# Six of eight units of a gate pair by seven products, a token sum in x's place, and a new order of the accumulating loads

## The chip, the cores and the metric

The kernel runs on one core of a Trainium2 chip. The time is device microseconds of one execution. A core has TensorE (PE, matmul; PEld is its weight load), VectorE (DVE), ScalarE (ACT), GpSimd (POOL) and SyncE (SP), each with its own instruction queue that runs in order. DMAs are issued here from SP's, ScalarE's and POOL's queues.

## What is computed

One layer of a decoder trunk on 256 tokens and 2048 features, in float32: a combined projection of the normed x, a short convolution branch and a gated recurrence branch, and then two sigmoid gates that merge the branches:

```python
h = rmsnorm(x, norm_mix_g[i])
u = h @ w_in[i]
...
m = jax.nn.sigmoid(ga) * (ya @ w_a_out[i]) + jax.nn.sigmoid(gb) * (yb @ w_b_out[i])
x = x + m @ w_o[i]
gate = jax.nn.sigmoid(rmsnorm(x, ple_norm_g[i]) @ w_ple_gate[i])
x = x + gate * (p[i] @ w_ple_proj[i])
```

ga and gb are two column ranges of u, 2048 columns each. The change is in how `h @ w_in` is computed for them.

## The kernel before

**Split operands.** A float32 product is made of three matmuls in the float32r format: each operand is cut in a high part (ScalarE copies it, rounded) and a low part (VectorE subtracts), and `triple` runs high x high, high x low and low x high. `cut` (L163 to L166) does this for a weight tile of 128 x 1024: `whi` by ScalarE, `wlo` by VectorE. x is cut once, into the two tiles of `state["hT"]` (16 slices of 128 features, 256 tokens each), which stay.

**Steps.** The projections run as a list of steps (`items`). A plain step takes one chunk of 256 features by 512 columns: 2 feature slices x 2 token halves x 3 = 12 matmuls. At step n the loop splits the weights of step n + 3 (`LEAD`), issues the matmuls of step n, issues loads up to step n + 7, and lets every open epilogue (a generator) go one step on. Weights come in tiles `raw` from SP's queue; the split pairs `whi`, `wlo` turn in four buffers.

**Pairs of gates.** The columns of ga and gb are done in four groups j of 512. After both gates of a j come the groups A and B (four plain steps each), whose results are multiplied in by `ep_a` and `ep_bb` and added into m. For j = 0 both gates are plain groups of eight steps. For the three later j the two gates are computed as a pair: a unit is one chunk of 256 features for both gates, so a product of a 2 x 2 block matrix (token halves by feature slices) with another (feature slices by gates). A unit with eight products is two steps of kind C, 12 matmuls each. A unit in `SEVEN` is one step of kind S that needs only seven products, 21 matmuls, by the scheme of Strassen and Winograd, but has sums of weights and of tokens as operands.

- Weights, `combine_weights` (L180): tile `sA` holds the unit's weights for ga, `sB` the second half of those for gb, both loaded from SP's queue (two buffers each). Tile `sT` holds the gb weights plus another block, and this sum is made by POOL's queue: a plain DMA, then an accumulating one (`add_by_dma`, three buffers). VectorE makes two sums in place in `sA` (L696), and three cuts follow: `thi`, `tlo` of sT (operands t1, t3), `bhi`, `blo` of sB (operand b22), `thi`, `tlo` of sA (t2, t4). The pairs `thi`, `tlo` turn in three buffers and `bhi`, `blo` has one. The plain split of sA into `whi`, `wlo` comes ahead of the sums. `combine_weights` for step n + 2 is issued at step n, ahead of the split of step n + 3.
- Tokens, `token_sums` (L730): for each unit in SEVEN, four sums s1 to s4 of the blocks of x are made and cut once, after group ga of j = 0, in groups of one or two units (`TOGETHER`), in a few steps of gb, A and B of j = 0; all three pairs use them.
- Products, `unit_products`: the seven go to the banks of `names_of`, in that order; `ep_products` and `ep_gates` put the banks together behind the last unit.

**Order.** From the end of ga of j = 0 until the end of the last B, `pinned` holds the instructions of ScalarE and of VectorE to the order in which the code issues them. In that order, at the last step of a group B, stand: the combination for step n + 2, the split of step n + 3, and then the four instructions of `ep_bb`, which wait for that step's matmuls. The end of a pair's last unit is followed directly by group A.

The other place that the change touches is `third_part`, in the third last step of the first group of W_o: it opens the tile for the sum x + m W_o, and `residual(0)` loads the first 512 columns of x into it from SP's queue.

Of the kernel before, what the change touches and what calls it, by code (L numbers as in the profile page):

```python
# [9 lines left out]
F32 = mybir.dt.float32  # L10
F32R = mybir.dt.float32r
AF = mybir.ActivationFunctionType
ALU = mybir.AluOpType
PSUM = bass.MemoryType.PSUM

P = 128
# [7 lines left out]
CW = 512  # L24
# [4 lines left out]
LB_MAX = 1.0 - 1e-6  # L29
SCAN = 64  # L30
LEVELS = [32, 16, 8, 4]
SEVEN = [()] + 3 * [(0, 2, 3, 5, 6)]
TOGETHER = [(0, 1), (1, 2), (3, 2)]
NARROW, Q = len(LEVELS), 32


# [11 lines left out]
def hybrid_kernel(ctx, tc, xT, x, pT, prm, gfin, masks, w_in, w_a, w_b, w_o, w_pg, w_pp, out):  # L48
    nc = tc.nc
# [9 lines left out]
    pools, closers = {}, {}  # L59

    def open_pool(name, side):
        closers[name] = ExitStack()
        pools[name] = closers[name].enter_context(
            tc.tile_pool(name=name, bufs=1, side=side, reuse_waits="tile")
        )

    def close_pool(name):
        closers.pop(name).close()
        del pools[name]
# [3 lines left out]
    state = {"tmp": "tmp1"}  # L73
# [3 lines left out]
    def nm(s):  # L77
        uid[0] += 1
        return f"{s}_{uid[0]}"
# [8 lines left out]
    def sc(n, tag="sc", bufs=12):  # L88
        return small.tile([P, n], F32, tag=tag, bufs=bufs, name=nm(tag))
# [6 lines left out]
    pair_sums = {}  # L96
# [9 lines left out]
    items = []  # L106
    for gi, (kind, j, w, g, op) in enumerate(groups):
        if kind == "gb" and SEVEN[j]:
            continue
        for c in range(w.shape[2]):  # L110
            it = {"gi": gi, "kind": kind, "j": j, "c": c, "last": c == w.shape[2] - 1}
            if kind != "ga" or not SEVEN[j]:
                key = ("PP", j // 2) if kind == "PP" else (gi, c // 2)
                items.append(dict(it, w=(w, g, c), raw=key, slot=(j if kind == "PP" else c) % 2))
            elif c in SEVEN[j]:
                items.append(dict(it, kind="S", w=(w, g, c), raw=(gi, c)))
# [6 lines left out]
    def raw_of(pos):  # L123
        it = items[pos]
        if it["raw"] not in loaded:
            if it["kind"] == "S":
                t = tuple(
                    pools["st"].tile([P, n, CW], F32, tag=tag, bufs=2, name=nm(tag)) for tag, n in (("sA", 2), ("sB", 1))
                )
            else:  # L130
                t = wp.tile([P, 2, 2 * CW], F32, tag="raw", bufs=3, name=nm("raw"))
            loaded[it["raw"]] = t
        return loaded[it["raw"]]
# [15 lines left out]
            else:  # L149
                nc.sync.dma_start(out=raw, in_=w[g, :, c : c + 2, :])  # L150

    def add_by_dma():
        pos = next((n for n, it in enumerate(items) if it["kind"] == "S" and n not in pair_sums), None)
        if pos is not None:
            w, g, c = items[pos]["w"]
            X = pair_sums[pos] = pools["st"].tile([P, 2, CW], F32, tag="sT", bufs=3, name=nm("sT"))
            nc.gpsimd.dma_start(out=X.rearrange("p n x -> p (n x)"), in_=w[g + 1, :, c, :])
            nc.gpsimd.dma_start(out=X, in_=w[g : g + 2, :, c, :CW].rearrange("n p x -> p n x"), accum_op=ALU.add)

    def pair_of(pool, n, tags=("whi", "wlo"), width=2 * CW):  # L160
        return tuple(pool.tile([P, width], F32R, tag=tag, bufs=n, name=nm(tag)) for tag in tags)
# [18 lines left out]
    def combine_weights(pos):  # L180
        st = pools["st"]
        (A, B), X = raw_of(pos), pair_sums[pos]
        add(A[:, 0], X[:, 0], B[:, 0])
        add(A[:, 1], A[:, 0], A[:, 1])
        ts = []
        for n, src in enumerate((X, B, A)):
            hi, lo = pair_of(st, 1, ("bhi", "blo"), CW) if n == 1 else pair_of(st, 3, ("thi", "tlo"))
# [9 lines left out]
    begun = next(n for n, it in enumerate(items) if it["kind"] == "ga" and it["last"])  # L197
# [7 lines left out]
    prm_t = const.tile([P, PRM_N], F32, name="prm_t")  # L205
    praw = pools["tmp1"].tile([P, 1024], F32, tag="X", bufs=4, name="praw")[:, : 2 * T]
    pop = pools["tmp1"].tile([P, 1024], F32R, tag="X", bufs=4, name="pop")
# [487 lines left out]
    def add(out, a, b):  # L695
        nc.vector.tensor_tensor(out=out, in0=a, in1=b, op=ALU.add)  # L696
# [32 lines left out]

    def token_sums():  # L730
        nu = len(SEVEN[1])
        state["S"] = pair_of(pools["st"], 1, ("shi", "slo"), nu * 4 * P)
        state["S"] = tuple(v.rearrange("p (u s t) -> p u s t", u=nu, s=4) for v in state["S"])
        for first, n in TOGETHER:
            for _ in range(3):
                yield
            F, S = (
                pools["st"].tile([P, 2 * CW], F32R, tag=tag, bufs=3, name=nm(tag))[:, : n * 4 * P].bitcast(F32)
                for tag in ("thi", "tlo")
            )  # L740
            c = SEVEN[1][first]
            hi, lo = (v[:, 2 * c : 2 * (c + n), :] for v in state["hT"])
            Fv = F.rearrange("p (k t) -> p k t", t=T)
            nc.vector.tensor_tensor(out=Fv, in0=hi.bitcast(F32), in1=lo.bitcast(F32), op=ALU.add)
            yield
            Fv = F.rearrange("p (u r b t) -> p u r b t", u=n, r=2, b=2)
            Sv = S.rearrange("p (u s t) -> p u s t", u=n, s=4)
            a11, a12, a21, a22 = Fv[:, :, 0, 0], Fv[:, :, 1, 0], Fv[:, :, 0, 1], Fv[:, :, 1, 1]
            s1, s2, s3, s4 = (Sv[:, :, i] for i in range(4))
            for out, u, v, op in (  # L750
                (s1, a21, a22, ALU.subtract), (s2, s1, a11, ALU.subtract),
                (s3, a11, a21, ALU.subtract), (s4, a12, s2, ALU.add),
            ):
                nc.vector.tensor_tensor(out=out, in0=u, in1=v, op=op)
            hi, lo = (v[:, first : first + n] for v in state["S"])
            nc.scalar.activation(out=hi, in_=Sv, func=AF.Copy)
            nc.vector.tensor_tensor(out=lo, in0=Sv, in1=hi.bitcast(F32), op=ALU.subtract)
            yield

    def ep_a(j, psum):  # L760
# [219 lines left out]
        open_pool("tmp2", "right")  # L980
        state["tmp"] = "tmp2"

    def residual(j):

        for t in range(NT):
            s = slice(j * CW, (j + 1) * CW)
            nc.sync.dma_start(out=state["x"][:, t, s], in_=x[:, t, s])

    def load_gfin():
        g = state["gfin"] = pools["tmp3"].tile([P, D], F32, name="gfin_t")  # L990
# [5 lines left out]
    def third_part():  # L996

        close_pool("tmp2")
        close_pool("branch")
        open_pool("tmp3", "right")  # L1000
        state["tmp"] = "tmp3"
        xs = pools["tmp3"].tile([P, NT, D], F32, name="xs")
        state["x"] = xs
        residual(0)
        state["ss2"] = sc(8, "ss2", 1)
        state["ss3"] = sc(12, "ss3", 1)
        nc.gpsimd.memset(state["ss3"].rearrange("p (t j) -> p t j", t=NT)[:, :, 5:6], EPS)
# [14 lines left out]
    def finish():  # L1022
        while active:
            advance()
# [24 lines left out]
    def names_of(it):  # L1049
        if it["kind"] == "C":  # L1050
            return [("c", it["n"], t) for i in range(2) for t in range(NT)]
        return ["P1", ("c", 0, 0), ("c", 1, 0), "P5", "P7", "P6", ("c", 0, 1)]

    def into(name, op, part):
        left[name] -= 1
# [3 lines left out]
    def unit_products(pos):  # L1059
        it = items[pos]  # L1060
        c, h = it["c"], state["hT"]

        def x_of(r, t):
            return tuple(v[:, 2 * c + r, t * P : (t + 1) * P] for v in h)

        hi, lo = parts.pop(pos)
        halves = [(hi[:, i * CW : (i + 1) * CW], lo[:, i * CW : (i + 1) * CW]) for i in range(2)]
        names = names_of(it)
        if it["kind"] == "C":
            for n, name in enumerate(names):  # L1070
                into(name, x_of(n // 2, n % 2), halves[n // 2])
            return
        b22, t1, t3, t2, t4_ = sums.pop(pos)
        s1, s2, s3, s4 = (tuple(v[:, SEVEN[1].index(c), i] for v in state["S"]) for i in range(4))
        for name, op, part in zip(names, (x_of(0, 0), x_of(1, 0), s4, s1, s3, s2, x_of(1, 1)),
                                  (halves[0], halves[1], b22, t1, t3, t2, t4_)):
            into(name, op, part)

    def pinned(start):
# [16 lines left out]
    for pos, it in enumerate(items[:last_group]):  # L1096
        mark = len(nc.cur_bb.bb.instructions)
        kind, j, c, last = (it[n] for n in ("kind", "j", "c", "last"))
        _, _, w, g, opname = groups[it["gi"]]
# [60 lines left out]
        else:  # L1160
            if c == 0:
                psum = [bank("s" if kind == "PP" and j >= 2 else "g") for _ in range(NT)]
            hi, lo = parts.pop(pos)
            for i in range(2):
                k = 2 * c + i
                s = slice(i * CW, (i + 1) * CW)
# [10 lines left out]
        if pos == begun:  # L1177
            finish()
            second_part()
            active.append(token_sums())  # L1180
            for _ in range(3):
                add_by_dma()
        if kind == "O" and j == 0 and c == nch - 3:
            finish()
            third_part()
# [22 lines left out]
    for t, halves in ((0, (0, 1)), (1, (0,)), (1, (1,))):  # L1208
        bk, n = bank("g"), CW // 2
        for c in range(nlast):  # L1210
# [3 lines left out]
            hi, lo = parts[last_group + c]  # L1214
            for i in range(2):
                k = 2 * c + i
                s = slice(i * CW + halves[0] * n, i * CW + (halves[-1] + 1) * n)
# [83 lines left out]
```

## Time and profile before

| | us |
|---|---|
| median of three runs | 818.3 (817.43 to 819.27) |
| the profiled execution | 818.19 |
| its span in the profile | 816.1 |
| granted TensorE clock, mean | 0.997 |

In the profile a row of a timeline is: start in us from the span's start, duration, engine, line, operation, out<-in, shapes, count, and in brackets the engine's idle time before it with what ended it. L165 is the subtraction in `cut`, L164 its copy, L1032 to L1034 the three matmuls of `triple`, L696 the sums of weights, L744 to L757 `token_sums`, L776 and L780 `ep_bb`, L141 the loads of sA and sB, L157 and L158 the plain and the accumulating DMA of sT. Before a pair's first unit TensorE is in group B of the j before; pair 1's first unit starts at 444.2 us, pair 2's at 508.1, pair 3's at 570.0.

### The profile page before, as it was taken

The page shows a single profiled execution, that of the slowest core. Times are in us where ns is not written, and L with a number is a line of the kernel's source. Part 1 is how long each engine was busy: PE and PEld are TensorE (multiplying, and loading weights), DVE is VectorE, ACT ScalarE, POOL GpSimd, SP SyncE. Part 2 cuts the span into 40 slices and gives each one's busy share as a digit, 9 for nine tenths or more (in the row PEclk, how much of TensorE's full clock was granted, in tenths as well). Part 3 has the DMA queues.
Part 4 walks back from the last instruction along what each step waited for, and adds up shares of the span by engine and source line. Part 5 has one row for each costly group of instructions (what it writes and reads, how often), then busy time and mean ns, then how long its engine had stood idle before and what let it go on. Part 6 is the DMA issues. An engine that isn't in the chain of part 4 may idle for free.

```text
span 816.1 us, 10646 instructions
## 1 busy us (share of the span) xinstructions
PE 804.2 (99%) x4059; PEld 664.6 (81%) x4059; DVE 589.0 (72%) x745; ACT 459.1 (56%) x614; POOL 49.2 (6%) x57
## 2 busy tenths in 40 slices
PE   9999999999999999999999999999999999999995
PEld 6888888888888888888888778888888788888885
DVE  6746588767766498766778988987988756677932
ACT  7576476465555466455545556556554546575623
POOL 1000000001000000012000110110100000001210
PEclk9999999999999999999999999999999999999998
DMA  9988555647867555649975898998944887796702
GB/s 334 396 302 287 198 205 169 235 138 270 253 235 250 198 175 195 206 161 327 350 246 194 243 290 289 291 276 260 278 171 174 299 283 281 250 343 267 275 35 103
DMA packets 52659, 198.52 MB, mean 243 GB/s; under 512 B 6784, under 2 KB 16256, under 8 KB 37888
## 3 DMA queue, kind: packets, MB, share of 16 engines
q1 hardware_dynamic: 45792, 181.07, 63.1%
q0 software_dynamic: 6240, 15.73, 8.3%
q10 hardware_dynamic: 576, 1.05, 0.4%
q8 instruction: 31, 0.51, 0.3%
q14 instruction: 20, 0.16, 0.1%
HBM read 184.19 MB, written 13.63 MB: 242 GB/s over the span
## 4 chain that ended last, share of the span: by engine, by line
PE 85%; DVE 7%; issue 3%; DMA 3%; ACT 2%; POOLq 0%; POOL 0%; DVEq 0%; ACTq 0%
PE g L1033 26%; PE g L1034 26%; PE g L1032 26%; DVE wlo L165 3%; PE s L1033 2%; PE s L1034 2%; PE s L1032 2%; DMA sA<-in_w_in 1%; DMA raw<-in_w_pp 1%; DVE tlo L165 1%; ACT whi L164 1%; DMA raw<-in_w_o 1%; DVE sA L696 1%; PE s L479 1%; DVE back L303 0%
## 5 line engine op out<-in xcount | busy, mean ns | idle before, releaser
L165 DVE TENSOR_TENSOR wlo<-raw,whi 128x1024 fp32r<-128x1024 f32 (+1 forms) x264 | 319.6, 1227 | 157.9 <-ACT whi L164 155.9
L164 ACT ACTIVATE whi<-raw 128x1024 fp32r<-128x1024 f32 (+1 forms) x264 | 272.8, 1049 | 205.0 <-PE g L1034 168.8
L1033 PE MATMUL g<-wlo,xh 128*128 128x512 f32 (+1 forms) x738 | 283.9, 385 | 0.0
L1034 PE MATMUL g<-whi,xl 128*128 128x512 f32 (+1 forms) x738 | 283.6, 385 | 0.0
L1032 PE MATMUL g<-whi,xh 128*128 128x512 f32 (+1 forms) x738 | 283.5, 385 | 0.0
L1033 PEld LDWEIGHTS g<-wlo,xh 128*128 128x128 f32 x738 | 138.7, 188 | 27.7 <-DVE wlo L165 0.3
L1032 PEld LDWEIGHTS g<-whi,xh 128*128 128x128 f32 x738 | 138.7, 188 | 27.4
L1034 PEld LDWEIGHTS g<-whi,xl 128*128 128x128 f32 x738 | 138.7, 188 | 27.4
L1033 PE MATMUL g<-wlo,mh 128*128 128x512 f32 x128 | 49.9, 390 | 0.3 <-DVE wlo L165 0.3
L1032 PE MATMUL g<-whi,mh 128*128 128x512 f32 x128 | 49.7, 389 | 0.0
L1034 PE MATMUL g<-whi,ml 128*128 128x512 f32 x128 | 49.5, 389 | 0.0
L1033 PE MATMUL s<-wlo,xh 128*128 128x512 f32 x84 | 32.7, 390 | 0.0
L1034 PE MATMUL s<-whi,xl 128*128 128x512 f32 x84 | 32.7, 389 | 0.0
L1032 PE MATMUL s<-whi,xh 128*128 128x512 f32 x84 | 32.5, 390 | 0.0
L164 ACT ACTIVATE thi<-sA 128x1024 fp32r<-128x1024 f32 x15 | 15.9, 1062 | 27.6 <-DVE sA L696 24.7
L1033 PEld LDWEIGHTS g<-wlo,mh 128*128 128x128 f32 x128 | 24.0, 188 | 5.7 <-DVE wlo L165 0.7
L1032 PEld LDWEIGHTS g<-whi,mh 128*128 128x128 f32 x128 | 24.0, 188 | 5.1
L1034 PEld LDWEIGHTS g<-whi,ml 128*128 128x128 f32 x128 | 24.0, 188 | 4.9
L1034 PE MATMUL g<-whi,ybTl 128*128 128x512 f32 x64 | 24.9, 389 | 0.0
L1033 PE MATMUL g<-wlo,ybTh 128*128 128x512 f32 x64 | 24.9, 389 | 0.0
L1032 PE MATMUL g<-whi,yaTh 128*128 128x512 f32 x64 | 24.9, 389 | 0.0
L1033 PE MATMUL g<-wlo,yaTh 128*128 128x512 f32 x64 | 24.9, 389 | 0.0
(215 smaller groups left out, 908.4 us busy)
## 6 DMA issues: line engine op xcount, KB each, us to landing
raw<-in_w_in SPq DMA_DIRECT2D x66, 1024.0 KB, 5.0
raw<-in_w_o SPq DMA_DIRECT2D x16, 1024.0 KB, 6.1
raw<-in_w_pg SPq DMA_DIRECT2D x16, 1024.0 KB, 5.6
sT<-in_w_in POOLq DMA_DIRECT2D x30, 512.0 KB, 7.4
raw<-in_w_in SPq DMA_DIRECT2D x28, 512.0 KB, 6.6
raw<-in_w_a SPq DMA_DIRECT2D x8, 1024.0 KB, 6.8
raw<-in_w_b SPq DMA_DIRECT2D x8, 1024.0 KB, 6.7
turn<-t SPq DMA_DIRECT2D x60, 128.0 KB, 3.0
```

The source lines that it names most:

```text
L164: a = nc.scalar.activation(out=hi, in_=src, func=AF.Copy)
L165: v = nc.vector.tensor_tensor(out=lo, in0=src, in1=hi.bitcast(F32), op=ALU.subtract)
L479: nc.tensor.matmul(out, X[:, 0, h, s], X[:, 1, h, t], start=True, stop=True, tile_position=(0, i * n))
L696: nc.vector.tensor_tensor(out=out, in0=a, in1=b, op=ALU.add)
L1032: nc.tensor.matmul(psum, oh, hi, start=first, stop=False)
L1033: nc.tensor.matmul(psum, oh, lo, start=False, stop=False)
L1034: nc.tensor.matmul(psum, ol, hi, start=False, stop=last)
```

## The change

SEVEN goes from units 0, 2, 3, 5, 6 to units 0, 1, 2, 4, 5, 6 in each later pair; units 3 and 7 keep eight products. The token sums are made in four groups (units 0 and 1; 2; 4 and 5; 6). Only s1 to s3 keep a tile of their own. s4 is cut into the slice of `hT` (even feature slice, second token half) that no seven-product unit reads. The first product of a unit is now s4 by b22, into another bank's place in the order; it was the third.

An addition by DMA is now spread over two calls: a call issues the plain load of one unit and, behind it, the accumulating DMA of the unit of the call before. sT has four buffers for three. The first calls come at four steps of gb and A of j = 0, each behind a ScalarE split, in place of three calls at the end of ga.

`residual(0)` issues its two loads from ScalarE's queue.

```diff
--- before.py
+++ after.py
@@ -29,8 +29,8 @@
 LB_MAX = 1.0 - 1e-6
 SCAN = 64
 LEVELS = [32, 16, 8, 4]
-SEVEN = [()] + 3 * [(0, 2, 3, 5, 6)]
-TOGETHER = [(0, 1), (1, 2), (3, 2)]
+SEVEN = [()] + 3 * [(0, 1, 2, 4, 5, 6)]
+TOGETHER = [(0, 2), (2, 1), (3, 2), (5, 1)]
 NARROW, Q = len(LEVELS), 32
 
 
@@ -149,13 +149,26 @@
             else:
                 nc.sync.dma_start(out=raw, in_=w[g, :, c : c + 2, :])
 
-    def add_by_dma():
+    def add_by_dma(behind=None):
         pos = next((n for n, it in enumerate(items) if it["kind"] == "S" and n not in pair_sums), None)
         if pos is not None:
             w, g, c = items[pos]["w"]
-            X = pair_sums[pos] = pools["st"].tile([P, 2, CW], F32, tag="sT", bufs=3, name=nm("sT"))
-            nc.gpsimd.dma_start(out=X.rearrange("p n x -> p (n x)"), in_=w[g + 1, :, c, :])
-            nc.gpsimd.dma_start(out=X, in_=w[g : g + 2, :, c, :CW].rearrange("n p x -> p n x"), accum_op=ALU.add)
+            X = pair_sums[pos] = pools["st"].tile([P, 2, CW], F32, tag="sT", bufs=4, name=nm("sT"))
+            d = nc.gpsimd.dma_start(out=X.rearrange("p n x -> p (n x)"), in_=w[g + 1, :, c, :])
+            if behind is not None:
+                tc.add_manual_dep(
+                    d.ins, behind.name,
+                    mybir.DependencyInfo(mybir.DependencyClass.Sync, mybir.DependencyReason.DATA), reason="order",
+                )
+        if "adding" in state:
+            w, g, c = items[state["adding"]]["w"]
+            X = pair_sums[state.pop("adding")]
+            with tc.issue_after(d.ins) if pos is not None else ExitStack():
+                nc.gpsimd.dma_start(
+                    out=X, in_=w[g : g + 2, :, c, :CW].rearrange("n p x -> p n x"), accum_op=ALU.add
+                )
+        if pos is not None:
+            state["adding"] = pos
 
     def pair_of(pool, n, tags=("whi", "wlo"), width=2 * CW):
         return tuple(pool.tile([P, width], F32R, tag=tag, bufs=n, name=nm(tag)) for tag in tags)
@@ -729,11 +742,12 @@
 
     def token_sums():
         nu = len(SEVEN[1])
-        state["S"] = pair_of(pools["st"], 1, ("shi", "slo"), nu * 4 * P)
-        state["S"] = tuple(v.rearrange("p (u s t) -> p u s t", u=nu, s=4) for v in state["S"])
+        state["S"] = pair_of(pools["st"], 1, ("shi", "slo"), nu * 3 * P)
+        state["S"] = tuple(v.rearrange("p (u s t) -> p u s t", u=nu, s=3) for v in state["S"])
+        yield
+        yield
         for first, n in TOGETHER:
-            for _ in range(3):
-                yield
+            yield
             F, S = (
                 pools["st"].tile([P, 2 * CW], F32R, tag=tag, bufs=3, name=nm(tag))[:, : n * 4 * P].bitcast(F32)
                 for tag in ("thi", "tlo")
@@ -752,9 +766,11 @@
                 (s3, a11, a21, ALU.subtract), (s4, a12, s2, ALU.add),
             ):
                 nc.vector.tensor_tensor(out=out, in0=u, in1=v, op=op)
-            hi, lo = (v[:, first : first + n] for v in state["S"])
-            nc.scalar.activation(out=hi, in_=Sv, func=AF.Copy)
-            nc.vector.tensor_tensor(out=lo, in0=Sv, in1=hi.bitcast(F32), op=ALU.subtract)
+            sums_of = tuple(v[:, first : first + n] for v in state["S"])
+            fourth = tuple(v[:, 2 * c : 2 * (c + n) : 2, P:] for v in state["hT"])
+            for (hi, lo), src in ((sums_of, Sv[:, :, :3]), (fourth, Sv[:, :, 3])):
+                nc.scalar.activation(out=hi, in_=src, func=AF.Copy)
+                nc.vector.tensor_tensor(out=lo, in0=src, in1=hi.bitcast(F32), op=ALU.subtract)
             yield
 
     def ep_a(j, psum):
@@ -980,11 +996,11 @@
         open_pool("tmp2", "right")
         state["tmp"] = "tmp2"
 
-    def residual(j):
+    def residual(j, queue=nc.sync):
 
         for t in range(NT):
             s = slice(j * CW, (j + 1) * CW)
-            nc.sync.dma_start(out=state["x"][:, t, s], in_=x[:, t, s])
+            queue.dma_start(out=state["x"][:, t, s], in_=x[:, t, s])
 
     def load_gfin():
         g = state["gfin"] = pools["tmp3"].tile([P, D], F32, name="gfin_t")
@@ -1001,7 +1017,7 @@
         state["tmp"] = "tmp3"
         xs = pools["tmp3"].tile([P, NT, D], F32, name="xs")
         state["x"] = xs
-        residual(0)
+        residual(0, nc.scalar)
         state["ss2"] = sc(8, "ss2", 1)
         state["ss3"] = sc(12, "ss3", 1)
         nc.gpsimd.memset(state["ss3"].rearrange("p (t j) -> p t j", t=NT)[:, :, 5:6], EPS)
@@ -1049,7 +1065,7 @@
     def names_of(it):
         if it["kind"] == "C":
             return [("c", it["n"], t) for i in range(2) for t in range(NT)]
-        return ["P1", ("c", 0, 0), ("c", 1, 0), "P5", "P7", "P6", ("c", 0, 1)]
+        return [("c", 1, 0), "P1", ("c", 0, 0), "P5", "P7", "P6", ("c", 0, 1)]
 
     def into(name, op, part):
         left[name] -= 1
@@ -1071,9 +1087,10 @@
                 into(name, x_of(n // 2, n % 2), halves[n // 2])
             return
         b22, t1, t3, t2, t4_ = sums.pop(pos)
-        s1, s2, s3, s4 = (tuple(v[:, SEVEN[1].index(c), i] for v in state["S"]) for i in range(4))
-        for name, op, part in zip(names, (x_of(0, 0), x_of(1, 0), s4, s1, s3, s2, x_of(1, 1)),
-                                  (halves[0], halves[1], b22, t1, t3, t2, t4_)):
+        s1, s2, s3 = (tuple(v[:, SEVEN[1].index(c), i] for v in state["S"]) for i in range(3))
+        s4 = x_of(0, 1)
+        for name, op, part in zip(names, (s4, x_of(0, 0), x_of(1, 0), s1, s3, s2, x_of(1, 1)),
+                                  (b22, halves[0], halves[1], t1, t3, t2, t4_)):
             into(name, op, part)
 
     def pinned(start):
@@ -1178,8 +1195,8 @@
             finish()
             second_part()
             active.append(token_sums())
-            for _ in range(3):
-                add_by_dma()
+        if pos in (begun + 3, begun + 5, begun + 7, begun + 9):
+            add_by_dma(state["splits"][0])
         if kind == "O" and j == 0 and c == nch - 3:
             finish()
             third_part()
```

## The prediction, made before the changed kernel was run

> **What bounds the kernel now.** I read the page first (busy shares, then the chain), then the stages of the three later pairs of gates by windows, then who waits for whom.
>
> ```profile
> span 816.1 us, 10646 instructions
> PE 804.2 (99%) x4059; PEld 664.6 (81%) x4059; DVE 589.0 (72%) x745; ACT 459.1 (56%) x614; POOL 49.2 (6%) x57
> PE 85%; DVE 7%; issue 3%; DMA 3%; ACT 2%; POOLq 0%; POOL 0%; DVEq 0%; ACTq 0%
> ```
>
> TensorE sets the end: 85% of the chain. VectorE's 72% is an average, so it is read where the change sits. The windows run from a pair's first unit to its last, and once over the groups A and B behind pair 2; columns: PE, PEld, DVE, ACT, POOL busy (instructions), clock, DMA share, GB/s.
>
> ```profile
> 444.20:486.40 42.20, 41.04 (x178) 32.92 (x177) 38.62 (x46) 22.20 (x25) 7.10 (x8) 1.00 0.89 265
> 508.10:548.30 40.20, 40.20 (x179) 33.26 (x179) 36.00 (x41) 21.88 (x26) 7.08 (x8) 1.00 0.94 286
> 548.30:570.00 21.70, 21.70 (x97) 18.00 (x96) 16.32 (x18) 12.83 (x15) 1.77 (x2) 1.00 0.84 260
> 570.00:610.20 40.20, 40.20 (x179) 33.26 (x179) 35.89 (x41) 21.79 (x26) 2.94 (x3) 1.00 0.70 221
> ```
>
> By the code each pair issues 5 x 21 + 6 x 12 = 177 matmuls here (the counts take in one or two at the edges). Pairs 2 and 3 do so without idle time: 40.20 / 177 = 0.227 us per matmul, 4.77 us for a seven-product step, 2.72 us for a step of twelve. Pair 1 takes 2.0 us more. These are its waits, and they are for VectorE:
>
> ```profile
> PE s L1033 <- DVE blo L165: 1.1, 1, 1.1
> PE s L1033 <- DVE wlo L165: 0.3, 1, 0.3
> ```
>
> So TensorE has no slack, and VectorE has 4 of 40 us. What counts is how early VectorE delivers each unit. Here are pair 2's first three seven-product units (units 0, 2, 3) on VectorE, then the rows of ScalarE that gate them:
>
> ```profile
> 501.29 1.23 DVE L165 TENSOR_TENSOR wlo<-sA,whi 128x1024 fp32r<-128x1024 f32 x1 [1.29 <-ACT whi L164]
> 502.55 0.69 DVE L696 TENSOR_TENSOR sA<-sT,sB 128x512 f32<-128x512 f32 x1
> 503.28 0.69 DVE L696 TENSOR_TENSOR sA<-sA 128x512 f32<-128x512 f32 x1
> 503.89 1.22 DVE L165 TENSOR_TENSOR tlo<-sT,thi 128x1024 fp32r<-128x1024 f32 x1
> 505.02 0.69 DVE L165 TENSOR_TENSOR blo<-sB,bhi 128x512 fp32r<-128x512 f32 x1
> 505.62 1.22 DVE L165 TENSOR_TENSOR tlo<-sA,thi 128x1024 fp32r<-128x1024 f32 x1
> 506.76 2.35 DVE L165 TENSOR_TENSOR wlo<-raw,whi 128x1024 fp32r<-128x1024 f32 x2
> 509.03 1.28 DVE L776 TENSOR_TENSOR gb<-gb,g 128x512 f32<-128x512 f32 x2
> 510.23 1.29 DVE L780 TENSOR_TENSOR t<-ga,gb 128x512 f32<-128x512 f32 x2
> 511.43 1.22 DVE L165 TENSOR_TENSOR wlo<-sA,whi 128x1024 fp32r<-128x1024 f32 x1
> ...
> 521.26 0.69 DVE L165 TENSOR_TENSOR blo<-sB,bhi 128x512 fp32r<-128x512 f32 x1 [0.57 <-ACT bhi L164]
> 523.05 1.23 DVE L165 TENSOR_TENSOR tlo<-sA,thi 128x1024 fp32r<-128x1024 f32 x1 [1.10 <-ACT thi L164]
> ```
> ```profile
> 500.20 1.06 ACT L164 ACTIVATE whi<-sA 128x1024 fp32r<-128x1024 f32 x1 [1.66 <-PE g L1034]
> ...
> 520.60 0.63 ACT L164 ACTIVATE bhi<-sB 128x512 fp32r<-128x512 f32 x1 [3.45 <-PE s L1034]
> ```
>
> Start to start, a unit costs VectorE 1.25 (wlo) + 0.73 + 0.61 (sums) + 1.14 + 0.60 + 1.14 (three low parts) = 5.47 us, and TensorE 4.77. A step of twelve costs VectorE 1.14 and TensorE 2.72. VectorE falls back by 0.7 us with each seven-product unit and gains 3.2 us with each eight-product one. It can't work ahead: 500.20 shows the first high part waiting for TensorE to leave the weight buffer used four steps earlier, and 520.60 shows the single bhi buffer waiting for the product of the unit before.
>
> **The change, part by part.**
>
> *Products.* In three pairs one unit goes from eight products to seven: 3 x 3 matmuls x 0.227 = 2.04 us off TensorE. Pair 1's 2.0 us of waits are taken out as well and counted anew below.
>
> *Three units in a row.* Units 1, 4, 7 had eight products; now 3 and 7. The row is now units 0, 1, 2, so the 3.2 us that unit 1 gave back between units 0 and 2 are gone. A unit's first product now takes b22, whose low part blo is the fourth VectorE instruction of the combination; it used to be the third product, 2 x 3 x 0.227 = 1.36 us later. The walk for pair 2, on the clock of the rows above, with unit 0's first product at 508.15:
> - unit 0 as before; the next instruction starts at 506.76.
> - wlo of unit 1 to 508.01; sums to 509.35; tlo to 510.49; blo to 511.09. The last thi waits for a ring of three buffers: free when unit 0's fifth product is done, 508.15 + 15 x 0.227 = 511.56, plus 0.24 to ScalarE and 1.10 on to VectorE: tlo 512.90 to 514.04.
> - wlo of unit 2 to 515.29. The four instructions of ep_bb (group B of the pair before) come next in program order, as at 509.03: 2.40, to 517.69.
> - unit 2: sums to 519.03, tlo to 520.17, blo ends 520.86.
> - TensorE reaches unit 2 at 508.15 + 2 x 4.77 = 517.69 and needs blo at 517.92. **Stall 3.0 us.**
>
> Going on, the two steps of unit 3 let VectorE catch up; units 4 and 5 arrive 2 us early, but unit 6, third of the next row, has blo at 541.1 and is needed at 540.6: 0.5 us. Pairs 2 and 3 so lose 3.5 us each.
>
> *Token sums.* Four groups in place of three; s4 is cut apart into the place of the operand that no seven-product unit reads any more.
>
> ```profile
> 414.02 0.28 DVE L754 TENSOR_TENSOR tlo<-thi 128x128 f32<-128x128 f32 x1
> 438.55 1.22 DVE L744 TENSOR_TENSOR thi<-xh,xl 128x1024 f32<-128x1024 f32 x1
> 447.70 1.23 DVE L757 TENSOR_TENSOR slo<-tlo,shi 128x1024 fp32r<-128x1024 f32 x1 [1.12 <-ACT shi L756]
> ```
>
> The added unit costs VectorE about 3 us (1.22 / 2 for the sum of its parts, four of 0.22 start to start, two low parts with their waits) in the steps of gb, A and B, which need 1.14 of every 2.72 us: hidden. The last group ends one step earlier: its sums and low part, 3.8 us up to 447.70 + 1.14 = 448.84, leave the midst of pair 1, but a one-unit group now stands ahead of the first combination: 0.9 us of sums, 0.65 of waiting for ScalarE and 0.8 of two low parts against the 1.14 of 438.55, so the combination starts at 440.9 in place of 439.69. Walked on: blo of unit 1 at 449.5 (needed 449.2: 0.3), unit 2's sA issued 445.2, landed 450.2 at the median below, ep_bb done 454.9, blo 458.1 against 454.3: 3.8. With unit 6's 0.5, pair 1 loses 4.6 us.
>
> *Accumulating DMAs.* POOL now issues the next plain load and right behind it the accumulating one, both at the end of a combination's first cut. POOL's own waiting goes, which nobody waited for. But both now lie ahead of unit 2's and unit 6's sA, which is issued 1.7 us later, when its buffer is free:
>
> ```profile
> 506.87 0.33 SPq L141 DMA_DIRECT2D sA<-in_w_in  x1
> DMA to landing us min/median/max: 4.1/5.0/10.6
> ```
> ```profile
> 461.36 1.17 POOL L158 DMA_DIRECT2D sT<-in_w_in  x1 [4.28 <-DMA sT<-in_w_in]
> 462.07 1.05 POOL L157 DMA_DIRECT2D sT<-in_w_in  x1
> 521.42 1.17 POOL L158 DMA_DIRECT2D sT<-in_w_in  x1 [5.29 <-DMA sT<-in_w_in]
> 522.13 1.06 POOL L157 DMA_DIRECT2D sT<-in_w_in  x1
> 463.40 8.67 DMA sA<-in_w_in
> ```
> ```profile
> sA<-in_w_in SPq DMA_DIRECT2D x1, 512.0 KB, 6.8
> ```
>
> The last line is the sA issued at 524.31, behind 521.42 and 522.13; the one at 463.40 took 8.67 us. Alone, the median is 5.0. Pair 2's unit 2 has a cover of 514.04 - 1.10 - 506.87 = 6.07 us, pair 1's none beyond 5.0, unit 6 some 5.9. The plain load now goes first, so I take 6.0, between the median and the nearer row of 6.8: 1.0 us, all in pair 1. Ends: nothing at 5.0; at 8.7, 3.7 + 2 x 2.6 + 2 x 2.8 = 14.5 us (unit 6 of pair 3 has nothing left to load beside it).
>
> *Initial additions* move from before group gb to its steps, behind a high part; the first sum is needed near 441, some 25 us later: nothing. *The first slice of x* goes from SP's queue to ScalarE's. Rows of the stage:
>
> ```profile
> 645.76 1.43 SPq L987 DMA_DIRECT2D xs<-in_x  x2
> 800.77 0.37 ACTq L904 DMA_DIRECT2D out<-xs  x1
> 651.81 1.06 ACT L164 ACTIVATE whi<-raw 128x1024 fp32r<-128x1024 f32 x1 [0.46 <-PE g L1034]
> ```
>
> Two issues are 0.8 us of ScalarE, which waits for TensorE there and is steps ahead; SP sheds 1.4 us. Between -0.6 and +0.8; I take nothing.
>
> **Sum** against the profiled run's own 818.2 us (span 816.1 and 2.1 around it; the median of the runs is 818.3): 818.2 - 2.0 - 2.0 + 4.6 + 3.5 + 3.5 + 1.0 = 826.8, so **827 us**, slower.
>
> **Rivals.**
>
> *VectorE is in time (not slower).* The verdict hangs on unit 2's blo. If ep_bb's 2.4 us ran behind the combination and the ring's 1.8 us of waiting fell away, blo would come at 516.7, before 517.9, and unit 6 would follow. Then only the gain is left: 818.2 - 4.0 = 814.2, or up to 818 where part of the stall stays. For it: pairs 2 and 3 lose nothing now, with two units in a row. Against: at 509.03 ep_bb stands ahead of the next combination.
>
> *The loads bound it.* DMA engines are 0.94 and 0.84 busy over pair 2, and each pair adds 0.75 MB net (1.75 for a unit of seven, 1.0 for one of eight). With sA at 8.7 us: 826.8 + 13.5 = 840.
>
> *The clock falls after a stall.* At the end TensorE is nearly idle and its clock drops:
>
> ```profile
> 470.00:480.00 10.00, 8.86 (x39) 7.04 (x38) 7.85 (x9) 6.57 (x8) 1.78 (x2) 1.00 0.99 311
> 806.00:816.00 10.00, 1.44 (x13) 1.23 (x11) 2.15 (x5) 2.32 (x5) 0.55 (x1) 0.75 0.29 105
> ```
> ```profile
> L926 PE MATMUL s<-warm 128*128 128x512 bf16 x8 | 3.6, 631 | 1.5 <-DVE warm L922 1.5
> ```
>
> A gap of 1.1 us (470 to 480) left it at 1.00. A mean of 0.75 over the last 10 us is half rate from 811 on, some 3.6 us after the last matmuls, which lie within 1.4 us of 806. At the start eight warming matmuls of 512 columns took 3.6 us, 0.45 each in place of 0.227: so long does the slow state last. A stall over 3.6 us, as pair 1's 3.8 may be, would then cost 1.8 us more: 828.6, or 832 if all three reach it. [...]
>
> *The write into x holds the readers.* If the tile were tracked whole, s4's write during gb would wait for all earlier readers and the next matmuls for it: ScalarE's and VectorE's short cuts, about 1 us, in two groups: 829.
>
> **How the numbers follow.** Forecast 0.56 (its own range 822 to 833); loads 0.16 (833 to 843); clock 0.06; the write 0.06; in time 0.16, of which 0.12 is faster by over 0.2% (1.6 us, about what a measurement can tell) and 0.04 within it. Slower 0.84. The range 817 to 838 leaves out the 0.12 and half of the loads.
>
> **What would show it.** TensorE idle on blo at unit 2 of each pair, 3 us or more, and about 0.5 at unit 6, with ep_bb ahead of that combination; 174 matmuls in a pair's stage of 42 to 45 us; unit 2's sA landing in 5 to 7 us; VectorE over 90% there. The prediction is wrong if blo of unit 2 is there before its step or if a pair's stage falls under 40.2 us.

## The result and the profile after

| | before | after |
|---|---|---|
| median, us | 818.52 (817.43 to 819.27, 6 runs) | 833.21 (830.36 to 835.76, 6 runs) |
| ratio to before, 95% interval | | 1.0182 (1.0166 to 1.0197) |
| profiled execution, its span | 818.19, 816.1 | 835.76, 834.0 |

The change makes the kernel slower, by 14.7 us in the medians; the forecast was 827, in a range of 817 to 838. These are the lines of the page of after that answer to the first ones of before: span, busy shares, chain.

```profile
span 834.0 us, 10691 instructions
PE 810.5 (97%) x4050; PEld 666.0 (80%) x4050; DVE 600.6 (72%) x767; ACT 464.7 (56%) x625; POOL 54.1 (6%) x63
PE 74%; DVE 13%; DMA 6%; issue 4%; ACT 3%; POOLq 0%; POOL 0%; DVEq 0%; ACTq 0%
```

The nine matmuls are gone (4050 for 4059), and still TensorE is busy longer and holds less of the chain, 74% for 85%; VectorE and the DMAs took what it lost. Here are windows in the three pairs and then the stretch behind them (the last B and the first group of W_o) of after, and that stretch of before (columns as in the prediction):

```profile
444.20:489.00 44.80, 39.71 (x162) 30.57 (x161) 37.64 (x42) 23.38 (x27) 10.45 (x12) 0.96 0.96 266
511.00:556.00 45.00, 41.34 (x177) 32.71 (x176) 38.63 (x44) 23.76 (x27) 10.77 (x12) 1.00 0.96 271
577.00:625.00 48.00, 45.45 (x193) 36.89 (x192) 41.87 (x49) 25.18 (x30) 4.81 (x5) 0.96 0.69 206
625.00:680.00 55.00, 52.96 (x225) 42.76 (x224) 38.73 (x38) 27.81 (x33) 0.00 (x0) 0.97 0.64 232
```
```profile
610.20:665.20 55.00, 54.72 (x241) 44.91 (x240) 40.12 (x39) 28.97 (x34) 0.00 (x0) 1.00 0.69 244
```

Subtract 0.227 us for each matmul of a window from its length: 44.80 - 162 x 0.227 = 8.0 us lost in pair 1, 4.8 in pair 2, 4.2 in pair 3, and 3.9 behind them (before: 55.00 - 241 x 0.227 = 0.3). Counted from start to start of the matmuls, without the windows' edges, it is 17.8 in the pairs (1.9 before) and 4.3 behind them (0.55 before). With the 2.0 us of the products: 816.1 - 2.0 + 15.9 + 3.75 = 833.8, against a span of 834.0. Below, "stalls" are counted in this second way, each time in the run that was profiled. VectorE is not at over 90% there, where I had expected it: 37.64 of 44.80 is 84%.

Who waits for whom, in the list of waits of after and then of before (total, times, longest):

```profile
ACT whi L177 <- DMA sA<-in_w_in: 17.4, 7, 4.1
...
ACT whi L177 <- DMA raw<-in_w_o: 6.7, 2, 4.7
...
PE s L1048 <- ACT whi L177: 4.9, 3, 2.7
PE s L1049 <- DVE blo L178: 3.7, 5, 1.7
PE s L1049 <- DVE wlo L178: 1.5, 2, 0.8
```
```profile
ACT whi L164 <- DMA sA<-in_w_in: 3.5, 2, 2.7
ACT whi L164 <- DMA raw<-in_w_o: 2.7, 1, 2.7
```

TensorE waits for blo, as forecast, but more for whi and wlo, which stand ahead of the sums. ScalarE makes whi, and it waits for the load of sA. Unit 2 of pair 2, as the chain of waits shows it (start, duration, what), and then on ScalarE and TensorE:

```profile
512.43 7.56 DMA sA<-in_w_in
519.99 0.02 issue
520.01 1.07 ACT whi L177
521.08 0.02 issue
521.11 1.22 DVE wlo L178
```
```profile
520.01 1.06 ACT L177 ACTIVATE whi<-sA 128x1024 fp32r<-128x1024 f32 x1 [1.64 <-DMA sA<-in_w_in]
...
521.12 0.50 PE L1048 MATMUL s<-whi,xh 128*128 128x512 f32 x1 [0.45 <-ACT whi L177]
522.38 0.50 PE L1049 MATMUL s<-wlo,xh 128*128 128x512 f32 x1 [0.76 <-DVE wlo L178]
...
525.92 0.39 PE L1048 MATMUL s<-bhi,xh 128*128 128x512 f32 x1
```

The load takes 7.56 us and everything behind it starts in the moment it lands. TensorE asks for unit 2's whi product first and comes to bhi at 525.92, where the code has its b22 product first: its order isn't the order of the code. Issue to landing of sA over the whole kernel was 4.1/5.0/10.6 before, and is now, by the view of the tile:

```profile
DMA to landing us min/median/max: 3.6/7.5/8.9
```

Two readings of this were open: VectorE is late in a row of three and the loads add a little (the forecast), or the loads are late and VectorE only passes that on.

### The profile page after: what moved, and what is told of

It is laid out like the page before. It is cut to its first block, busy times and chain, and to the rows that moved or that the text cites. A ratio compares the mean times of both kernels' runs of the same rounds, so it can differ in the third digit from the quotient of the medians.

```text
span 834.0 us, 10691 instructions
## 1 busy us (share of the span) xinstructions
PE 810.5 (97%) x4050; PEld 666.0 (80%) x4050; DVE 600.6 (72%) x767; ACT 464.7 (56%) x625; POOL 54.1 (6%) x63
## 4 chain that ended last, share of the span: by engine, by line
PE 74%; DVE 13%; DMA 6%; issue 4%; ACT 3%; POOLq 0%; POOL 0%; DVEq 0%; ACTq 0%
PE g L1049 23%; PE g L1048 23%; PE g L1050 23%; DMA sA<-in_w_in 5%; DVE wlo L178 4%; DVE tlo L178 3%; DVE sA L709 2%; ACT whi L177 1%; DMA raw<-in_w_o 1%; PE s L1049 1%; PE s L1050 1%; DVE gb L792 1%; PE s L1048 1%; PE s L492 1%; PE s L942 0%
## 5 line engine op out<-in xcount | busy, mean ns | idle before, releaser
L178 DVE TENSOR_TENSOR wlo<-raw,whi 128x1024 fp32r<-128x1024 f32 (+1 forms) x258 | 312.6, 1228 | 162.8 <-ACT whi L177 161.0
L177 ACT ACTIVATE whi<-raw 128x1024 fp32r<-128x1024 f32 (+1 forms) x258 | 266.6, 1050 | 210.8 <-PE g L1050 175.4
L177 ACT ACTIVATE thi<-sA 128x1024 fp32r<-128x1024 f32 x18 | 19.1, 1063 | 35.3 <-DVE sA L709 25.5
L178 DVE TENSOR_TENSOR wlo<-sA,whi 128x1024 fp32r<-128x1024 f32 x18 | 22.0, 1222 | 16.5 <-ACT whi L177 16.5
L1048 PE MATMUL s<-whi,xh 128*128 128x512 f32 x72 | 28.6, 401 | 4.9 <-ACT whi L177 4.9
L177 ACT ACTIVATE whi<-sA 128x1024 fp32r<-128x1024 f32 x18 | 19.0, 1055 | 22.3 <-DMA sA<-in_w_in 17.4
L1049 PE MATMUL s<-wlo,xh 128*128 128x512 f32 x72 | 28.9, 401 | 1.6 <-DVE wlo L178 1.5
L1050 PE MATMUL s<-whi,xl 128*128 128x512 f32 x72 | 28.3, 393 | 0.0
```

The source lines that it names most:

```text
L177: a = nc.scalar.activation(out=hi, in_=src, func=AF.Copy)
L178: v = nc.vector.tensor_tensor(out=lo, in0=src, in1=hi.bitcast(F32), op=ALU.subtract)
L1048: nc.tensor.matmul(psum, oh, hi, start=first, stop=False)
L1049: nc.tensor.matmul(psum, oh, lo, start=False, stop=False)
L1050: nc.tensor.matmul(psum, ol, hi, start=False, stop=last)
```

## The experiments

All edits are made on the changed kernel. Times are medians of the kernel's runs, ratios are to the kernel before on the same chip.

**One relief at a time.** e1 puts the accumulating DMA back behind its own plain load, e2 loads the first slice of x from SP's queue again, e3 makes the b22 product the third again.

```diff
e1:      d = nc.gpsimd.dma_start(out=X..., in_=w[g + 1, :, c, :])
+        nc.gpsimd.dma_start(out=X, in_=w[g : g + 2, :, c, :CW]..., accum_op=ALU.add)
...
e2: -    residual(0, nc.scalar)
    +    residual(0)
e3: -    [("c", 1, 0), "P1", ("c", 0, 0), "P5", "P7", "P6", ("c", 0, 1)]
    +    ["P1", ("c", 0, 0), ("c", 1, 0), "P5", "P7", "P6", ("c", 0, 1)]
```

> The changed kernel, but each accumulating DMA is issued right behind its own plain load and waits for it on POOL, as before the change; the rest as changed. If the two POOL DMAs ahead of each sA make it late: sA lands again in about 5 us (7.5 in the changed kernel), ScalarE's wait for sA falls from 17.4 us to under 5, TensorE's stalls in the three pairs fall from 18 us (clock drops included) to 9 to 12, and the time is 825 to 829. If VectorE's queue alone sets the stalls (three units in a row, ep_bb ahead of the third), the wait for sA goes but the time stays above 831.

> The changed kernel, but the first slice of x is loaded from SP's queue as before. If moving it to ScalarE's queue caused the new stall in the first group of W_o (4.2 us of TensorE, 0.6 before): that stall is back under 1 us and the time falls by 2 to 4 us, to about 830. If it comes from the late start of that group's weight load behind the turn of m: the stall stays at 2 to 4 us and the time at 831 to 835.

> The changed kernel, but s4 by b22 is the third product of a unit again, not the first. By the walk blo is then needed 1.36 us later: TensorE's waits for blo (3.7 us) go and the time falls by 1 to 3 us. Rival: the single bhi buffer is held 1.36 us longer, the next unit's combination waits for it, and the time is the same or up to 3 us longer.

| run | median us (range) | ratio (interval) | stalls in the pairs, behind them |
|---|---|---|---|
| after | 833.21 (830.36 to 835.76) | 1.0182 (1.0166 to 1.0197) | 17.8, 4.3 |
| e1 | 829.46 (824.66 to 833.85) | 1.0137 (1.0081 to 1.0192) | 9.9, 2.5 |
| e2 | 832.22 (831.10 to 834.12) | 1.0174 (1.0156 to 1.0192) | 16.1, 2.7 |
| e3 | 833.10 (831.31 to 834.42) | 1.0175 (1.0157 to 1.0193) | 16.0, 5.1 |

e1's runs lie in two heaps (824.7 and 825.7, 833.3 and 833.9), and the stalls are those of a run of the lower one. sA lands in 5.2 us there, and ScalarE still waits 11.9 us for it, where under 5 was expected. e2 and e3 do nothing that can be measured: no cost of the first slice of x shows, and none of the place of b22, for which I had reckoned up to 1.36 us a unit. (e2's 2.7 behind the pairs is about after's 4.3 less the 1.7 of the drop of the clock that after has there, at 666 us.)

**The row.** e4 takes five units, 0, 2, 3, 5, 6, with all the rest of the change; e9 takes five others, three of them in a row.

```diff
-SEVEN = [()] + 3 * [(0, 1, 2, 4, 5, 6)]
-TOGETHER = [(0, 2), (2, 1), (3, 2), (5, 1)]
e4: +SEVEN = [()] + 3 * [(0, 2, 3, 5, 6)]
    +TOGETHER = [(0, 1), (1, 2), (3, 2)]
e9: +SEVEN = [()] + 3 * [(0, 1, 2, 4, 5)]
    +TOGETHER = [(0, 2), (2, 1), (3, 2)]
```

> The changed kernel with the five units 0, 2, 3, 5, 6 by seven products as before (token sums in three groups); s4 in place of x, the order of the products, the DMAs and the load of x stay as changed. If the sixth unit and its three in a row are the cause: no stall over 1 us in pairs 2 and 3, none over 1.5 in pair 1, a time of 816 to 821. If the late sA is a cause by itself: sA lands in 7 us or more here too and TensorE still stalls 3 us or more in the pairs, time 822 or more.

> Five units by seven products, as in the run with units 0, 2, 3, 5, 6 (815.4 us, no stall in the pairs), but units 0, 1, 2, 4, 5: as many products, weight sums, loads and token sums, only with three units in a row. If three in a row is what costs: TensorE stalls 2 to 4 us in each pair between unit 0 and unit 3, none or little at units 4 and 5, and the time is 822 to 829. If the sixth unit's load on VectorE and the DMA engines is what costs: stalls under 1 us a pair, 815 to 818.

e4: 815.41 us (815.33 to 815.47), ratio 0.9968 (0.9955 to 0.9981), stalls 0.0 in the pairs and 0.6 behind them. It is faster than both kernels. e9: 827.96 (826.42 to 828.28), ratio 1.0115 (1.0100 to 1.0130), stalls 9.3 and 1.9. Both have the same numbers of matmuls, cuts and loads; three in a row alone make 12.5 us in the medians. sA lands as late in e4 (median 7.6) as in e9 (7.4): with two in a row it harms nothing.

**Relief for VectorE and for the buffers.** e5 lets ep_bb's two additions run one step later. e6 is e1 with a third buffer for sA, paid for by sT's fourth. e8 is both.

```diff
e5, in ep_bb:
         m = t4()
+        if j < 3:
+            yield
...
e6: -    tag=tag, bufs=2, ... for tag, n in (("sA", 2), ("sB", 1))
    +    tag=tag, bufs=n + 1, ... for tag, n in (("sA", 2), ("sB", 1))
    -    tag="sT", bufs=4
    +    tag="sT", bufs=3
```

> The changed kernel, but the two adds of ep_bb (1.2 us of VectorE) come one step later, behind unit 2's combination. If VectorE's queue at unit 2 sets the stall: up to 1.2 us less in each pair, fewer clock drops, time 827 to 831. If the late sA alone sets it: the same stalls, 832 to 835.

> Six units; each accumulating DMA behind its own plain load (as in the run of 829.5 us), sT with three buffers and sA, sB with one more each, so that sA is loaded a unit earlier. ScalarE's wait for sA goes to nearly nothing. If VectorE's queue sets the rest: stalls of 7 to 10 us in the pairs stay, 823 to 829. If the loads set it: stalls under 4 us, 815 to 820.

> As the run with the extra sA and sB buffers, with ep_bb's adds one step later as well. By VectorE's queue 2 to 4 us less than that run, 820 to 826, and still more than the 815.4 of five units. If six can be carried: under 815.

e5: 832.22 (828.65 to 834.84), no difference from after that its runs could show; stalls 20.1 and 1.9, in its slowest run. e6: 828.26 (826.05 to 831.78), stalls 11.3 and 1.2. Only sA has a buffer more there; sB keeps its two, other than the expectation says. e8: 831.00 (828.48 to 833.41), 13.0 and 2.6; what was expected of it, 820 to 826, did not come. By its time alone e6 would speak for VectorE (823 to 829 was expected then), but in its list of waits sA is gone, and this stands in its place:

```profile
ACT thi L169 <- DMA sT<-in_w_in: 14.7, 4, 5.8
DVE sA L701 <- DMA sT<-in_w_in: 8.0, 3, 4.0
PE s L1040 <- ACT bhi L169: 6.0, 3, 3.6
```

With a buffer more sA is in time, and now sT is late; bhi stands behind thi of sT on ScalarE, and TensorE waits for bhi. The wait has only changed its tile, and both tiles are loads. sT has a buffer less here than in after, so its lateness can come from that too.

**Loads or VectorE.** e10 leaves VectorE and TensorE all their work and takes loads away: sA and sB are loaded for the first two units of pair 1 only, and the later units compute with these weights. e11 leaves the loads and takes 1.14 us of VectorE from each unit. e7 asks which part of the change gave e4 its gain.

```diff
e10, load():
-    for n, to in enumerate(raw):
+    for n, to in enumerate(raw if len(state["kept"]) < 3 else ()):
...
e11, combine_weights():
+    if n == 2:
+        nc.scalar.activation(out=hi, in_=src..., func=AF.Copy)
+        lo = first
e7: e4 and e1 and e2 together
```

> The changed kernel with six units, but the tiles sA and sB are loaded only for the first two units of pair 1 and then kept: the later seven-product units split and sum what stands there. Left out are 16 of 18 loads of 512 KB and 16 of 18 of 256 KB; every instruction of TensorE, VectorE and ScalarE stays, and the sums of sT still come by DMA. Theory A (VectorE's order and work: its third unit in a row comes late whatever the loads do): the stalls in the pairs stay at 8 to 12 us of the 17.8, and the time is 823 to 828. Theory B (the loads: sA lands 7.5 us after its issue in place of 5.0, and the chain whi, wlo, sums, cuts starts that much too late): the stalls fall under 2 us and the time is 813 to 816. Both together: 816 to 822, with what is left waiting for blo or wlo.

> The changed kernel with six units, but the low part of the third cut (tlo of sA, for t2 and t4) is not made: the products take tlo of sT in its place. VectorE has 1.14 us less for each of 18 units, so 4.33 us a unit against TensorE's 4.77; loads, ScalarE and the matmuls stay. Theory A (VectorE): the stalls in the pairs fall from 17.8 to under 4 us, and the time is 814 to 820. Theory B (the loads): the late sA holds whi and wlo as before, the stalls stay over 10 us and the time is over 825. Both together: 820 to 825.

> Five units (0, 2, 3, 5, 6) with the rest of the change, except that the accumulating DMA goes directly behind its own plain load again and the first slice of x is loaded from SP's queue. e4_five, with the new order of the DMAs, took 815.41, 2.6 us under the kernel before; its pairs had no stalls. If that gain comes from the token sums and the order of the products (pair 1's 2.0 us of waits are gone because the tokens' last group ends a step earlier): 815 to 816 again. If it comes from the new order of the DMAs: 817.5 to 818.5, with about 2 us of waits in pair 1.

e10: 818.39 us (816.91 to 820.05, 10 runs), ratio 1.0005 (0.9994 to 1.0015), stalls 2.2 in the pairs, none of them over 0.5, and 2.35 behind them. The row of three is there, ep_bb stands where it stood, and TensorE goes through all its matmuls in the same order as in after; only the loads are gone, and with them 15.6 us of stalls. Pairs 2 and 3 of e10 by windows of 20 us:

```profile
520.00:540.00 20.00, 20.00 (x90) 16.49 (x89) 19.80 (x23) 13.68 (x17) 6.03 (x7) 1.00 0.93 222
580.00:600.00 20.00, 19.94 (x88) 16.16 (x87) 19.80 (x23) 13.67 (x17) 0.00 (x0) 1.00 0.27 84
```

VectorE is busy for 19.80 of 20 us, and TensorE waits for nothing. The row of three fills VectorE to the brim, but with the loads in time it costs at most the 2.2 us that are left in the pairs. By what was expected, e10 lies at the edge: its stalls are just over the "under 2" of the loads alone, and its time, 818.39, is in the range of both causes together, 2.35 us of it behind the pairs.

e11: 826.47 (823.53 to 827.65), ratio 1.0089 (1.0063 to 1.0115), stalls 12.8 and 0.7. By what was expected (over 825, stalls over 10) that is the theory of the loads. But 5 us are gone, and it doesn't decide how much of them is VectorE's, since the subtraction that it leaves out was also the last reader of sA: in pair 2, unit 2's sA is issued 4.9 us after unit 0's whi in place of 6.7. The stalls at unit 2 are gone, and unit 6, whose sA lands in 10.1 and 9.1 us in pairs 1 and 2, has nearly all of the 12.8, with some 10 us of half clock in it (mean clock 0.94, 0.89 and 0.91 over 460 to 480, 480 to 500 and 540 to 560 us). So it stays open whether late loads would cost less if VectorE, with next to no idle time in the row, could catch up.

e7: 816.02 (815.05 to 821.62, 10 runs), ratio 0.9980 (0.9965 to 0.9996), no stall in the pairs. With sA landing in 5.5 us it is no faster than e4: the gain of the five is not from the new order of the DMAs but from the rest of the change, the token sums and the order of the products, which I didn't part.

**Six without the row.**

```diff
+    for j in (1, 2, 3):
+        a = next(n for n, it in enumerate(items) if it["j"] == j and it["kind"] in ("S", "C"))
+        u = items[a : a + 10]
+        items[a : a + 10] = [u[n] for n in (0, 1, 3, 2, 5, 4, 6, 7, 8, 9)]
```

> The changed kernel with the same six seven-product units in each later pair, the same matmuls, cuts and loads, but the two steps of unit 3 are taken apart: the pair runs as units 0, 1, the first gate of 3, units 2, 4, the second gate of 3, units 5, 6, and unit 7. So no three seven-product steps stand in a row; a row of two asks the DMA engines for 3.5 MB, the row of three for 5.25. If the row is the cause (three units' loads within 14.3 us, which lands the third unit's sA late), the stalls in the pairs fall from 17.8 to under 5 us and the time is 813 to 819; without any stall it is 813.4, e4_five's 815.4 less nine matmuls. If the whole number of loads of a pair is the cause (12.5 MB in 38 us), the stalls stay at 8 us or more, the time is over 823.

826.18 us (825.06 to 829.17), ratio 1.0107 (1.0078 to 1.0136), stalls 10.6 and 2.7, ScalarE's wait for sA 15.7. So the row is a part, and not all: seven us go, but six units stall without it too. That was expected if the whole number of loads of a pair is too much. This is how full the DMA engines are in e4's first two pairs, where nothing stalls:

```profile
441.00:481.00 40.00, 40.00 (x178) 33.14 (x177) 37.24 (x42) 22.98 (x26) 8.98 (x10) 1.00 1.01 303
505.00:545.00 40.00, 40.00 (x178) 33.14 (x177) 36.32 (x42) 21.04 (x24) 7.18 (x8) 1.00 1.03 314
```

With five units they are at a share of 1.0 and move 303 to 314 GB/s, so 12.1 to 12.6 MB in 40 us. A sixth adds 0.75 MiB (0.79 MB) and leaves 0.7 us less, three matmuls of a pair (the 38 us in e13's expectation is wrong): 12.9 to 13.4 MB in 39.3 us, 328 to 340 GB/s. At 314 that takes 41.1 to 42.5 us, an estimate of 1.8 to 3.2 us lost in each of the first two pairs, whatever the order. This rate belongs to this mix of loads: in W_o after moves 376 GB/s at a share of 0.94 (window 660 to 667 us).

The time of the engines says the same without a rate. By the packets of after (their durations stand in the last section) a unit of seven products takes (128 x 159 + 128 x 84 + 128 x 159 + 256 x 176) / 16 = 6032 ns of the 16 engines, 6.0 us against 4.77 of TensorE, and a unit of eight 2.5 against 5.44. Five and three make 37.8 us against TensorE's 40.2, six and two 41.3 against 39.5; three in a row take 18.1 us against 14.3. Without sA and sB, as in e10, a unit of seven takes 4.1 us. These are estimates that leave out all other loads.

e1, e6 and e13, the best with six, lost 2.8, 1.8 and 3.7 us in pair 2, about as much as these estimates say, but 4.8, 9.1 and 6.8 in pair 1. What pair 1 loses beyond stays open.

## Why the prediction came out as it did

The side and the range were right. The forecast was 6 us low, and its largest term stood on the wrong cause: that it came this near is in good part luck, since 11.6 us that did not come stood in for those that the loads cost. Term by term, in us against the profiled execution before:

| term | predicted | measured |
|---|---|---|
| nine matmuls | -2.0 | -2.0 |
| pair 1's old waits | -2.0 | -1.9 |
| VectorE in the row of three, pairs 1 to 3 | +4.6 +3.5 +3.5 | at most 2.2 by itself (e10) |
| sA later (measured: all stalls of the pairs without the clock) | +1.0 | +14.4 |
| clock after stalls | a rival | +5.1 |
| behind the pairs | 0 | +2.1 |

**Products and pair 1's waits.** Right. e4, which has these parts of the change without the sixth unit, has no stall in any pair.

**Three units in a row.** The row was the right place and VectorE the wrong reason. VectorE's walk itself was good; these are e10's rows for unit 0's first product, unit 2's blo, and the product that takes it:

```profile
506.62 0.39 PE L1053 MATMUL s<-bhi,xh 128*128 128x512 f32 x1
```
```profile
518.45 0.69 DVE L183 TENSOR_TENSOR blo<-sB,bhi 128x512 fp32r<-128x512 f32 x1
```
```profile
519.40 0.40 PE L1054 MATMUL s<-blo,xh 128*128 128x512 f32 x1
```

The walk had blo 520.86 - 508.15 = 12.7 us after unit 0's first product; here it is 518.45 + 0.69 - 506.62 = 12.5. What failed is the step by which TensorE reaches unit 2 at 517.69 "and needs blo at 517.92", 9.8 us after unit 0's first product. TensorE asked for it at 12.8. `pinned` holds ScalarE and VectorE to the order of the code, not TensorE, and the products of units 0 to 2 are interleaved: unit 2's whi products come early, its b22 products are drawn out. That took up the 3.0 us of the stall. I had read the order of two engines from the code and then taken it for the third. The rows of before would not have shown it: there, and in e4, with two in a row at most, TensorE goes through the seven products of a unit in the order of the code. That b22's place (e3) and ep_bb (e5) made no difference fits this.

**sA's landing.** The mechanism was named (two POOL loads stand ahead of unit 2's and unit 6's sA), and so was the rival "the loads bound it", at a chance of 0.16. The step that failed is "I take 6.0, between the median and the nearer row of 6.8": the median came to 7.5. The upper end of this term, 14.5 us at 8.7, is about what was lost: 17.8 us of stalls in the pairs less two clock drops of 1.7. But that is partly luck, since at 7.5 the prediction's own covers give 2.5 + 2 x 1.43 + 2 x 1.6 = 8.6. The rest fits a VectorE that was full and could not make up for what came late; no run shows this alone. The rival's 840 was too high by VectorE's 11.6 us, which were counted beside it; without them and with the clock and the stretch behind it is 836. I had the DMA share of 0.94 in the rows and did not divide it through: a sixth unit adds 0.75 MiB net to engines that are nearly full and takes 0.7 us away.

**The clock.** It was set at stalls over 3.6 us, an estimate from two rows of before, and did come, at shorter ones (the longest wait of TensorE there was 2.7): three drops to half clock of 3.41 us in the profiled execution, 1.7 us lost in each. Its runs from 830.4 at a mean clock of 0.998 to 835.8 at 0.991 fit that.

**Behind the pairs.** Nothing was forecast there. 2.1 us beyond the clock are lost in the last B and the first group of W_o, where ScalarE waits 6.7 us for loads of W_o, 2.7 before. The first slice of x is not the cause (e2), nor are sA and sB (e10 has 2.35). What it is stays open.

**The write into x, the first additions, VectorE in time.** No stall shows at the token sums (gb, A and B before pair 1 have none). "VectorE is in time" held where the loads were in time (e10, up to the 2.2 us left), but not its 814.2, since the loads stalled the changed kernel instead.

**Open.** Whether sA is late for its bytes or for its time of issue (two buffers) is parted only so far: e6 took the second away for sA, and sT, which had lost a buffer, became late. The packets' times speak for the bytes, as an estimate. Reducing sT's loads alone was not tried.

## What to carry to other kernels

Before a faster algorithm takes more operands, divide the bytes of a stage by its new, shorter time, and compare that with what the DMA engines move where their share is near 1: here a unit of seven products asks for 1.75 MiB in 4.77 us, 385 GB/s, where e4's first two pairs moved 303 to 314. The mix of loads must be the same, or the sum be made in engine time: here 2 KB accumulated took 176 ns of an engine and 2 KB plain 84. An order that the code sets for some engines need not hold for the others (TensorE asked for blo at 12.8 us where the code's order had 9.8); read TensorE's own rows of the changed kernel before an operand is called late. Where a stall has two possible feeders, take one away whole (the loads, in e10): reliefs of one us here and there moved the wait from tile to tile and told little.

## What the runs showed of the hardware

**The clock dropped behind stretches of 3.41 us that TensorE spent mostly waiting, not idle throughout.** Windows of after: the stretch ahead of each of its three drops between the first pair and W_o, and the drop; then a stretch that TensorE spent half waiting.

```profile
451.00:454.40 3.40, 0.70 (x4) 0.28 (x3) 0.13 (x1) 1.22 (x2) 0.15 (x1) 1.00 1.07 336
454.40:457.80 3.40, 3.27 (x7) 2.12 (x8) 3.40 (x5) 1.30 (x2) 0.00 (x0) 0.50 1.10 282
...
587.49:590.90 3.41, 1.33 (x5) 0.88 (x6) 2.11 (x3) 2.53 (x3) 1.03 (x1) 1.00 1.10 270
590.90:594.30 3.40, 3.40 (x10) 2.63 (x9) 3.37 (x6) 0.46 (x1) 0.18 (x1) 0.51 0.99 199
...
662.58:665.99 3.41, 1.37 (x5) 0.78 (x5) 1.82 (x2) 2.01 (x2) 0.00 (x0) 1.00 1.00 417
665.99:669.40 3.41, 3.41 (x10) 2.64 (x9) 2.89 (x3) 1.06 (x1) 0.00 (x0) 0.51 0.65 202
```
```profile
539.73:543.14 3.41, 1.70 (x9) 1.08 (x7) 3.34 (x6) 1.42 (x2) 0.38 (x1) 1.00 1.07 342
```

TensorE was busy for 0.70, 1.33 and 1.37 of 3.4 us, and the next 3.41 us ran at half the clock, which is 1.7 us lost each time; it was busy for 1.70, and no drop followed. In the clock records of after's trace each of the three drops is 3.413 us long; 133.12 and 71.68 us at full clock lie between them and 160.43 behind the third, up to the one at the kernel's end: 39, 21 and 47 times 3.413. Cut into such stretches from the drops on, 430 to 690 us of after has no other one in which TensorE was busy for less than 1.70. In the stretch from 587.49 the waiting was in two pieces, of 1.80 and 0.76 us by its waits. What sets off a drop, beyond these, no run shows.

**In after, an accumulated byte took over twice the engine time of a plain one.** Medians of the packets in its trace: an accumulating load's packet of 2 KB takes 176 ns, one of 2 KB on SP's queue 84; a plain packet of 4 KB takes 159 on POOL's queue and 159 on SP's. The queues' totals, in packets, MB and share of 16 engines, hide it, since POOL's queue holds plain and accumulating loads of sT in equal parts:

```profile
q1 hardware_dynamic: 45504, 179.76, 61.1%
q0 software_dynamic: 7488, 18.88, 9.7%
```

POOL's queue takes 0.51% of the engines' span for a MB and the other 0.34%. sA lands in 7.5 us (after) and 7.6 (e4), where a plain and an accumulating load of 512 KB are issued mostly within 1.5 us ahead of it, and in 5.2 (e1) and 5.5 (e7), where the accumulating one waits for its own plain load. Which of the two loads ahead makes it late was not tried.
